# The gate product of the first half of each row tile: GpSimd in place of VectorE, in the transition behind the dilated attention

## The chip, the cores and the metric

The kernel runs on one core of one Trainium2 chip. A core has five engines with queues of their own: TensorE (PE in the profile, its weight loads PEld), VectorE (DVE), ScalarE (ACT), GpSimd (POOL) and SyncE (SP), which here issues the DMAs. The metric is device time in microseconds for one execution, the median of several runs.

## The reference

The kernel computes two decoder layers on a sequence of 512 rows of width 1024 in float32. Each layer is feed-forward, token mixer, feed-forward; the mixer of layer 0 is latent attention, that of layer 1 is dilated attention. Every one of the six sub-layers is wrapped in the same way:

```
hn = rmsnorm(x, pre_g) * (1 + scale) + shift
y  = rmsnorm(fn(hn), post_g)
x  = x + res_w * gate * y
```

So at the end of a sub-layer each row of its output y needs the mean of its squares, a product with the 1024 gates (gate, post_g and res_w folded into one row), a factor of its own (the inverse root of that mean) and a sum with x. Then the next sub-layer's norm takes the mean of squares of the new x, and its inverse root. The change touches the product with the gates alone.

## The kernel before, in words

Every float32 weight or activation that enters a matmul is split into a high part (ScalarE) and a low part (VectorE, a subtraction), and three matmuls make up one product (`mm3`, lines 149 to 151). The lines of these splits are 134 and 136 for weights (67 and 71 where they come in two halves) and 711 and 712 for the last attention outputs.

Rows are cut into four tiles of 128 (i = 0 to 3), the width into two halves of 512 (d = 0, 1). A transition between two sub-layers goes through the tiles in order:

- `tail(i)` has TensorE do the last products of tile i, for both halves, in PSUM; `y_part` adds them on VectorE to the part made earlier (line 465), into `y[i][d]` in SBUF.
- `y_done(i, d)` squares the half on ScalarE with a sum over the row (line 316), and multiplies the half in place by the gates `gb` (line 477, VectorE). The square reads y before the product overwrites it.
- `tile_done(i)`: `scale_of` adds the two sums on VectorE (line 323) and raises the result to the power -0.5 on GpSimd (line 324, 128x1). Then VectorE does x = y * r + x for both halves (line 505).
- `normal(i)`: both halves of the new x are squared (line 316), the same `scale_of` follows, and the normed rows are written by ScalarE (half 0, line 339) and VectorE (half 1, line 340).
- `turn`: for each pair of tiles, TensorE transposes the normed rows (line 529), and `modulate` scales and splits them on VectorE and ScalarE (lines 311 to 313; two columns out of eight by ScalarE and GpSimd, lines 307 to 309). The first matmuls of the next sub-layer need these.

Around the transition, ScalarE and VectorE also split the first weights of the next feed-forward sub-layer.

The program is written with a framework that traces the instructions, plans their order on each engine by priorities and cost estimates of its own, and sets the semaphores. `high_priority(offset=HOT)` (400) raises the steps of `y_part` and `y_done`, twice that those of `scale_of`. In the dilated sub-layer's main part the order of TensorE, ScalarE and VectorE is the written one; in the transition behind it only that of SyncE is, and the other four queues are planned. On each engine instructions run in the planned order.

`busy` is a class attribute: True for the dilated mixer alone, False for the latent one; the feed-forward class calls `y_done` on its own. In `Mixer.tail` the step of the change is the last line:

```python
t.y_part(i, d, b, False)
t.y_done(i, d)
```

Of the kernel before, what the change touches and what calls it, by code (L numbers as in the profile page):

```python
# [10 lines left out]
ALU = mybir.AluOpType  # L11
# [4 lines left out]
SEQ = 512  # L16
# [60 lines left out]
class Trunk:  # L77
# [390 lines left out]
            else:  # L468
                nc.scalar.activation(y, b, AF.Copy)

    def y_done(self, i, d):
        with self.tc.high_priority(offset=HOT):
            if d == 0:
                self.ss = self.pair()
            y = self.y[i][d]
            self.square(y, self.t("sq", SB), self.ss[:, d : d + 1])
            self.nc.vector.tensor_tensor(y, y, self.gb[:, d * SEQ : (d + 1) * SEQ], ALU.mult)

    def transition(self, sub, nxt):
        for u in (sub, nxt):  # L480
# [57 lines left out]
class Ffn:  # L538
# [89 lines left out]
    def tail(self, i):  # L628
        self.down(len(GROUPS) - 1, i)
# [34 lines left out]
class Mixer:  # L664
# [30 lines left out]
    def tail(self, i):  # L695

        t = self.t
        if i == 0:
            self.open = {(q, d): t.bank() for q in range(self.waiting) for d in range(2)}
            for (q, d), b in self.open.items():  # L700
                self.products(b, q, d, range(self.early, KT - 1))
        for d in range(2):
            b = self.open.get((i, d)) or t.bank()
            self.products(b, i, d, range(KT - 1 if (i, d) in self.open else self.early, KT))
            t.y_part(i, d, b, False)
            t.y_done(i, d)

    def put_o(self, src):
        t, nc = self.t, self.t.nc
# [915 lines left out]
```

## Time and profile before

| quantity | value |
|---|---|
| median of 3 runs (lowest, highest) | 2249.92 us (2248.58, 2249.99) |
| the profiled execution's own time | 2249.64 us |
| its span in the trace | 2247.9 us |
| TensorE busy, granted clock | 2217.0 us (99%), 0.997 |
| VectorE busy | 1181.0 us (53%) |
| ScalarE busy | 847.8 us (38%) |
| GpSimd busy | 108.6 us (5%) |

The profile is that of one execution. The transition behind the dilated sub-layer lies at about 1855 to 1890 us of its span. A row of the timeline has the start in us, the length in us, engine, line, operation, output<-inputs, shapes and a count; in brackets stands how long the engine sat idle before it, and what ended that. Two instructions that follow each other on VectorE or ScalarE overlap by some 0.08 to 0.1 us, so the distance from start to start is shorter than the length.

### The profile page before, as it was taken

How to read it: one execution, taken by the hardware profiler on the slowest of the kernel's cores; microseconds unless marked ns; L12 is line 12 of the kernel's file. 1: busy time of each engine (PE TensorE's matmuls, PEld its weight loads, DVE VectorE, ACT ScalarE, POOL GpSimd, SP SyncE). 2: the span in 40 equal slices, each digit the busy share in tenths (PEclk: the TensorE clock that was granted, in tenths of full speed). 3: DMA queues.
4: the chain of work that ended last, by engine and by line, in shares of the span. 5: the costliest groups of instructions: out<-in, count | busy, mean ns of one | idle time of the engine just before them, and what ended most of it. 6: DMA issues, size and time to landing. Idle time of an engine off the chain costs nothing.

```text
span 2247.9 us, 30150 instructions
## 1 busy us (share of the span) xinstructions
PE 2217.0 (99%) x11354; PEld 1868.2 (83%) x11354; DVE 1181.0 (53%) x2691; ACT 847.8 (38%) x1730; POOL 108.6 (5%) x143
## 2 busy tenths in 40 slices
PE   7999999999999999999999999999999999999998
PEld 5888888877898888898888889888899888888887
DVE  7666565677665456574554464234523457333344
ACT  4432234578633132353222353425442446322232
POOL 0000001210110000020000010000000002000000
PEclk9999999999999999999999999999999999999999
DMA  8575762311155365434644523323342334233231
GB/s 309 161 243 185 199 216 74 108 55 57 61 167 185 113 180 178 138 111 132 190 167 133 159 92 108 111 90 97 85 130 68 104 81 143 90 118 100 77 112 38
DMA packets 124058, 290.34 MB, mean 129 GB/s; under 512 B 44787, under 2 KB 49158, under 8 KB 123911
## 3 DMA queue, kind: packets, MB, share of 16 engines
q1 hardware_dynamic: 123910, 288.41, 40.8%
q8 instruction: 89, 1.46, 0.3%
q14 instruction: 59, 0.48, 0.1%
HBM read 281.76 MB, written 4.49 MB: 127 GB/s over the span
## 4 chain that ended last, share of the span: by engine, by line
PE 89%; ACT 2%; DVE 2%; issue 2%; DMA 2%; POOL 1%; SPq 1%; POOLq 0%; DVEq 0%; ACTq 0%
PE mm L149 28%; PE mm L150 28%; PE mm L151 27%; PE mm L882 1%; PE aux L1297 1%; PE mm L1130 1%; PE aux L931 1%; PE aux L1264 1%; POOL mv L324 1%; PE aux L910 1%; PE aux L529 0%; DVE wlo L136 0%; DMA z<-dz 0%; ACT whi L134 0%; DMA d<-w 0%
## 5 line engine op out<-in xcount | busy, mean ns | idle before, releaser
L136 DVE TENSOR_TENSOR wlo<-raw,whi 128x512 fp32r<-128x512 f32 (+1 forms) x714 | 466.1, 690 | 593.1 <-ACT whi L134 588.9
L149 PE MATMUL mm<-s,whi 128*128 128x512 f32 (+1 forms) x1932 | 722.6, 375 | 1.5 <-ACT whi L134 1.5
L150 PE MATMUL mm<-s,whi 128*128 128x512 f32 (+1 forms) x1932 | 719.1, 372 | 0.0
L151 PE MATMUL mm<-s,wlo 128*128 128x512 f32 (+1 forms) x1932 | 718.7, 372 | 0.0
L134 ACT ACTIVATE whi<-raw 128x1024 fp32r<-128x1024 f32 (+1 forms) x357 | 369.3, 1048 | 786.5 <-PE mm L150 540.7
L149 PEld LDWEIGHTS mm<-s,whi 128*128 128x128 f32 x1932 | 364.6, 189 | 68.9 <-issue 3.5
L151 PEld LDWEIGHTS mm<-s,wlo 128*128 128x128 f32 x1932 | 364.5, 189 | 63.6
L150 PEld LDWEIGHTS mm<-s,whi 128*128 128x128 f32 x1932 | 364.8, 189 | 61.8
L149 PE MATMUL mm<-whi,s 128*128 128x512 f32 (+1 forms) x1040 | 406.4, 391 | 1.7 <-ACT s L711 1.7
L150 PE MATMUL mm<-wlo,s 128*128 128x512 f32 (+1 forms) x1040 | 404.4, 389 | 0.0
L151 PE MATMUL mm<-whi,s 128*128 128x512 f32 (+1 forms) x1040 | 404.2, 389 | 0.0
L149 PEld LDWEIGHTS mm<-whi,s 128*128 128x128 f32 x1040 | 210.8, 203 | 37.2 <-ACT s L711 2.1
L151 PEld LDWEIGHTS mm<-whi,s 128*128 128x128 f32 x1040 | 210.8, 203 | 34.5 <-DVE s L712 0.2
L150 PEld LDWEIGHTS mm<-wlo,s 128*128 128x128 f32 x1040 | 210.9, 203 | 33.8 <-issue 0.3
L171 DVE CUSTOM_DVE_ANT_0 raw<-raw,cs 128x1024 f32<-128x1024 f32 x130 | 160.0, 1235 | 123.2 <-DMA raw<-w_mod 122.6
L465 DVE TENSOR_TENSOR s<-mm,s 128x512 f32<-128x512 f32 x112 | 76.6, 689 | 119.0 <-PE mm L151 118.8
L324 POOL TENSOR_TENSOR mv<-mv,mhalf 128x1 f32<-128x1 f32 x48 | 36.1, 755 | 1486.9 <-DVE mv L323 1484.4
L1095 ACT ACTIVATE s<-mm 128x128 f32<-128x128 f32 (+3 forms) x109 | 33.2, 360 | 165.2 <-PE mm L151 161.3
L588 ACT ACTIVATE s<-gg 128x512 fp32r<-128x512 f32 (+1 forms) x97 | 57.4, 592 | 44.8 <-DVE gg L587 44.8
L587 DVE TENSOR_TENSOR gg<-silu,mm 128x512 f32<-128x512 f32 (+1 forms) x95 | 59.8, 629 | 9.3 <-ACT silu L585 9.3
L585 ACT ACTIVATE silu<-mm 128x512 f32<-128x512 f32 (+1 forms) x95 | 51.4, 541 | 18.1 <-PE mm L151 18.1
L1211 ACT ACTIVATE u<-u,y 128x128 f32<-128x128 f32 x128 | 49.6, 397 | 22.1 <-DVE y L1189 10.0
(185 smaller groups left out, 1686.4 us busy)
## 6 DMA issues: line engine op xcount, KB each, us to landing
raw<-w_gu SPq DMA_DIRECT2D x168, 512.0 KB, 4.2
raw<-w_mod SPq DMA_DIRECT2D x130, 512.0 KB, 4.6
raw<-w_down SPq DMA_DIRECT2D x88, 512.0 KB, 4.4
raw<-dil_in SPq DMA_DIRECT2D x47, 512.0 KB, 4.1
raw<-dil_v SPq DMA_DIRECT2D x20, 512.0 KB, 4.5
s<-w_mod SPq DMA_DIRECT2D x28, 256.0 KB, 6.0
raw<-w_gu SPq DMA_DIRECT2D x16, 256.0 KB, 3.8
raw<-mla_o SPq DMA_DIRECT2D x8, 512.0 KB, 3.9
```

The lines of the kernel that those rows point to most:

```text
L134: self.nc.scalar.activation(hi, raw, AF.Copy)
L136: self.nc.vector.tensor_tensor(lo[:, r], raw[:, r], f(hi[:, r]), ALU.subtract)
L149: mm(out, w[0], m[0], start=first, stop=False)
L150: mm(out, w[0], m[1], start=False, stop=False)
L151: mm(out, w[1], m[0], start=False, stop=last)
L171: nc.vector.tensor_tensor_reduce(raw, raw, self.cs, 1.0, 0.0, ALU.mult, ALU.add, accum_out=t[:, 0:1])
L324: nc.gpsimd.tensor_tensor(v[:, 1:2], v[:, 0:1], self.mhalf[:, 0:1], ALU.pow)
L465: nc.vector.tensor_tensor(y, b, y, ALU.add)
L585: nc.scalar.activation(s, banks[0], AF.Silu)
L587: nc.vector.tensor_tensor(v, s, banks[1], ALU.mult)
L588: nc.scalar.activation(ghi, v, AF.Copy)
L1211: nc.scalar.activation(c, c, AF.Exp, bias=pair["top"][:, g, i, one], scale=-1.0, accum_out=pair["z"][:, g, i, one],)
```

## The change

`y_done` gets a flag, and with it the product with the gates is issued on GpSimd in place of VectorE. `Mixer.tail` sets it for half 0 where `busy` is true, which is the dilated mixer: four instructions of 128x512 in all, one for each row tile. Half 1 and everything else stays.

```diff
-    def y_done(self, i, d):
+    def y_done(self, i, d, spare=False):
         with self.tc.high_priority(offset=HOT):
             if d == 0:
                 self.ss = self.pair()
             y = self.y[i][d]
             self.square(y, self.t("sq", SB), self.ss[:, d : d + 1])
-            self.nc.vector.tensor_tensor(y, y, self.gb[:, d * SEQ : (d + 1) * SEQ], ALU.mult)
+            eng = self.nc.gpsimd if spare else self.nc.vector
+            eng.tensor_tensor(y, y, self.gb[:, d * SEQ : (d + 1) * SEQ], ALU.mult)
...
             t.y_part(i, d, b, False)
-            t.y_done(i, d)
+            t.y_done(i, d, self.busy and d == 0)
```

## Rows read from the trace of the kernel before

**Rows 1.** The page: busy time of the engines over the whole span, and the share of each in the chain that ended last.

```profile
PE 2217.0 (99%) x11354; PEld 1868.2 (83%) x11354; DVE 1181.0 (53%) x2691; ACT 847.8 (38%) x1730; POOL 108.6 (5%) x143
...
PE 89%; ACT 2%; DVE 2%; issue 2%; DMA 2%; POOL 1%; SPq 1%; POOLq 0%; DVEq 0%; ACTq 0%
```

**Rows 2.** Busy time in stretches of the transition: the stretch, its length, then busy us (and instructions) of PE, PEld, DVE, ACT and POOL, the granted clock of TensorE, the DMA share and GB/s.

```profile
1860.00:1870.00 10.00, 10.00 (x47) 8.28 (x46) 9.84 (x18) 8.75 (x22) 1.57 (x3) 1.00 0.43 150
1870.00:1880.00 10.00, 5.67 (x32) 5.03 (x31) 9.76 (x23) 9.27 (x22) 4.26 (x5) 0.83 0.39 126
...
1878.00:1879.00 1.00, 1.00 (x7) 1.00 (x6) 1.00 (x3) 1.00 (x4) 0.53 (x1) 0.50 0.73 246
1879.00:1880.00 1.00, 1.00 (x7) 1.00 (x7) 1.00 (x3) 1.00 (x4) 1.00 (x1) 0.61 0.02 8
```

**Rows 3.** Timeline of TensorE: the two instructions of 1860 to 1890 us before which it sat idle.

```profile
1872.04 1.53 PE L529 MATMUL aux<-ident,s 128*128 128x128 f32 x12 [1.64 <-ACT s L339]
1876.27 0.73 PE L149 MATMUL mm<-s 128*128 128x256 f32 x2 [2.69 <-ACT s L312]
```

**Rows 4.** Groups of VectorE's instructions from 1855 to 1890 us: the product with the gates (busy us, mean ns).

```profile
L477 DVE TENSOR_TENSOR s<-s,gb 128x512 f32<-128x512 f32 x8 | 5.2, 684 | 0.0
```

**Rows 5.** Timeline of VectorE in the transition, tiles 0 to 2.

```profile
1859.21 0.15 DVE L323 SCALAR_TENSOR_TENSOR mv<-ss 128x1 f32<-128x1 f32 x1
1859.28 0.68 DVE L477 TENSOR_TENSOR s<-s,gb 128x512 f32<-128x512 f32 x1
1859.88 0.68 DVE L465 TENSOR_TENSOR s<-mm,s 128x512 f32<-128x512 f32 x1
1860.48 1.41 DVE L505 SCALAR_TENSOR_TENSOR x<-s,mv,x 128x512 f32<-128x512 f32 x2
...
1862.40 0.68 DVE L71 TENSOR_TENSOR s<-raw,s 128x512 fp32r<-128x512 f32 x1
1863.00 1.28 DVE L477 TENSOR_TENSOR s<-s,gb 128x512 f32<-128x512 f32 x2
1864.21 0.22 DVE L323 SCALAR_TENSOR_TENSOR mv<-ss 128x1 f32<-128x1 f32 x2
1864.51 0.69 DVE L465 TENSOR_TENSOR s<-mm,s 128x512 f32<-128x512 f32 x1
...
1867.60 0.69 DVE L465 TENSOR_TENSOR s<-mm,s 128x512 f32<-128x512 f32 x1
1868.20 0.69 DVE L136 TENSOR_TENSOR wlo<-raw,whi 128x512 fp32r<-128x512 f32 x1
1868.80 1.29 DVE L477 TENSOR_TENSOR s<-s,gb 128x512 f32<-128x512 f32 x2
1870.00 0.22 DVE L323 SCALAR_TENSOR_TENSOR mv<-ss 128x1 f32<-128x1 f32 x2
```

**Rows 6.** Timeline of ScalarE in the same stretch: the squares of half 0 of tiles 0, 1 and 2, the normed rows of tile 1, and the first high parts for the next sub-layer.

```profile
1857.59 0.63 ACT L316 ACTIVATE sq<-s 128x512 f32<-128x512 f32 x1 [2.10 <-DVE s L465]
...
1861.88 0.62 ACT L316 ACTIVATE sq<-s 128x512 f32<-128x512 f32 x1
...
1867.37 0.62 ACT L316 ACTIVATE sq<-s 128x512 f32<-128x512 f32 x1
...
1871.27 0.72 ACT L339 ACTIVATE s<-x,mv 128x512 f32<-128x512 f32 x1 [0.50 <-POOL mv L324]
...
1875.82 0.71 ACT L312 ACTIVATE s<-u 128x256 fp32r<-128x256 f32 x2
```

**Rows 7.** Timeline of GpSimd in the same stretch: all it does there up to 1876 us.

```profile
1859.44 0.93 POOL L324 TENSOR_TENSOR mv<-mv,mhalf 128x1 f32<-128x1 f32 x1 [95.53 <-DVE mv L323]
1864.43 1.20 POOL L324 TENSOR_TENSOR mv<-mv,mhalf 128x1 f32<-128x1 f32 x2 [4.07 <-DVE mv L323]
1870.24 1.62 POOL L324 TENSOR_TENSOR mv<-mv,mhalf 128x1 f32<-128x1 f32 x2 [4.61 <-DVE mv L323]
```

**Rows 8.** GpSimd elsewhere: the group of the products with sines in the latent attention (same shape and type; count, busy us, mean ns), and one subtraction of half the width behind the transition.

```profile
L830 POOL TENSOR_TENSOR s<-s 128x512 f32<-128x512 f32 x4 | 5.1, 1283 | 69.1 <-DVE s L828 64.1 <-issue 5.0
...
1903.94 0.74 POOL L590 TENSOR_TENSOR s<-gg,s 128x256 fp32r<-128x256 f32 x1 [5.08 <-ACT s L588]
```

**Rows 9.** Timelines of GpSimd and VectorE at two other places where both work on SBUF at once: at 54 us (GpSimd 128x512), and at 993 us (GpSimd 128x256).

```profile
54.54 0.68 DVE L190 CUSTOM_DVE_ANT_0 s<-s,cs 128x512 f32<-128x512 f32 x1
55.15 1.78 DVE L190 CUSTOM_DVE_ANT_0 s<-s,cs 128x512 f32<-128x512 f32 x1
54.84 1.54 POOL L309 TENSOR_TENSOR s<-u,s 128x512 fp32r<-128x512 f32 x1 [11.84 <-ACT u L308]
...
993.88 0.68 DVE L136 TENSOR_TENSOR wlo<-raw,whi 128x512 fp32r<-128x512 f32 x1
994.48 1.21 DVE L171 CUSTOM_DVE_ANT_0 raw<-raw,cs 128x1024 f32<-128x1024 f32 x1
995.63 1.75 DVE L171 CUSTOM_DVE_ANT_0 raw<-raw,cs 128x1024 f32<-128x1024 f32 x1
993.55 2.75 POOL L590 TENSOR_TENSOR s<-gg,s 128x256 fp32r<-128x256 f32 x1 [2.77 <-ACT s L588]
```

**Rows 10.** Timeline of SyncE's queue behind the last product: the gates of the next sub-layer, then the next weights.

```profile
1876.05 0.33 SPq L246 DMA_DIRECT2D gb<-row  x1
1879.53 4.91 SPq L124 DMA_DIRECT2D raw<-w_gu  x2
```

## The prediction

> **What bounds the kernel now.** I read the page first: TensorE is busy in 2217.0 of 2247.9 us and holds 89% of the chain that ended last [rows 1]. So a change that adds or removes no matmul counts only where TensorE stands. I then went to the one place where the four products lie, and cut it into stretches: from 1860 to 1870 us TensorE is full, from 1870 to 1880 it works 5.67 of 10 us, while VectorE is at 9.84 and 9.76 and ScalarE at 8.75 and 9.27 [rows 2]. Here VectorE and ScalarE set the pace. TensorE's own timeline shows the two waits: 1.64 us until the normed rows of tile 1 are written by ScalarE, and 2.69 us until the first high part for the next sub-layer is there, together 4.33 us [rows 3]. Behind the second wait the granted clock is at its lower level, 1.2 GHz (0.50 in 1878 to 1879), and returns during 1879 to 1880 [rows 2]; from the restart at 1876.27 to about 1879.7 half the time, some 1.7 us, is lost as well. So 4.33 + 1.7 = 6.0 us is the most that any repair of this place can win.
>
> What releases the first wait can be followed backwards in the timelines: the normed rows (1871.27) stood behind a power on GpSimd (1870.24) [rows 6, 7], that behind the tiny sum of line 323 on VectorE (1870.00), and that behind the two gate products of tile 2 (1868.80) [rows 5]. The same pattern stands at tile 1: two products at 1863.00, the sum at 1864.21, the power at 1864.43 [rows 5, 7].
>
> **The change part by part.**
>
> *Removed from VectorE.* Four products of 128x512. One lasts 684 ns [rows 4], but two in a row take 1.20 us from the first's start to the next instruction (1868.80 to 1870.00 [rows 5]), so a place in the queue is worth 0.60 us, four 2.4 us. Only those of tiles 1 and 2, 1.2 us, stand directly ahead of a sum on the way to the restart. Tile 0's would give 0.6 more if all behind it moved up. Tile 3's lies behind the work that releases TensorE and is worth nothing.
>
> *Added on GpSimd.* Four products with three operands in SBUF. The nearest row has the same shape, type and operation: 1283 ns [rows 8]. So one product is 0.6 us longer than on VectorE (1.28 against 0.68), and GpSimd has the time: between 1859 and 1876 it did nothing but powers [rows 7]. Two costs follow.
>
> *The power behind the product.* The product can start when the square of half 0 is done. ScalarE starts it at 1857.59, 1861.88 and 1867.37 for tiles 0 to 2, 0.62 us each [rows 6]; the square of half 1 follows within a further 0.8 us or less (0.61 and the reading of the sum), and then the power could run. In GpSimd's queue it stands behind a product of 1.28 us. With nothing else in the way it is late by 1.28 - 0.8 = 0.5 us a tile. What waits for the power is line 505, and through it everything of that tile.
>
> *VectorE and GpSimd at the same memory.* At 54.84 us GpSimd runs a 128x512 subtraction. The VectorE instruction that starts at 55.15 takes 1.78 us in place of the 0.68 of its neighbour and ends 0.55 us after GpSimd does (56.93 against 56.38): it stood still until GpSimd was through. GpSimd too was stretched, to 1.54 us, while VectorE's earlier instruction finished [rows 9]. At 993.55 us VectorE runs without a gap, and a GpSimd instruction of half our width takes 2.75 us in place of 0.74 [rows 8, 9]: it waited some 2.0 us before it got its turn, and then VectorE's instruction took 1.75 for 1.21 us.
>
> The Trainium skill states this as a lock (SBUF — State Buffer, "Who interferes with whom"): a VectorE instruction with two SBUF inputs and a GpSimd instruction that reads SBUF take the shared port pair for the whole instruction, and the second to issue blocks. The first half agrees with the 1.78 us [rows 9]; by the page GpSimd would wait for one VectorE instruction, by the row at 993.55 it waited for several. With one such wait of 0.69 us at tiles 1 and 2 the sum would be 2 x (0.69 + 1.28 - 0.60) = 2.7 us slower, 2252.3.
>
> So the 0.60 us that VectorE saves can be lost again: its remaining product, the sums and lines 71, 136 and 505 read two operands from SBUF. Line 465 reads one from PSUM; no row of before shows it beside a GpSimd product. From both sides: if it runs on, 0.60 of the 1.28 us are covered where it comes at the right moment; if not, nothing is. I take that it runs on. For one tile VectorE's balance is then between -0.60 (nothing stops) and 1.28 - 0.60 = +0.68 us (all stops).
>
> *The sum, tile by tile.* Tile 0: product on GpSimd from about 1858.35 to 1859.65. VectorE's product of half 1 stands until then and ends its place at 1860.25, line 465 at 1860.85, and line 505 starts there in place of 1860.48 [rows 5]: +0.4. Tile 1: ScalarE's square starts 0.4 later and ends at 1862.9. GpSimd comes in behind line 71, at 1863.4, and is through at 1864.7. VectorE's product of half 1 takes until 1865.3, the power starts at 1865.5 in place of 1864.43 [rows 5, 7]: +1.1. Tile 2: the square ends at about 1868.7 (ScalarE had 0.3 us of other work to spare), just under line 465, so GpSimd gets in at 1868.75 and ends at 1870.05. Line 136 and the product of half 1 follow, two places of 0.60, and the power that was at 1870.24 starts at 1871.4 to 1871.5: +1.2. From there to the restart ScalarE's queue runs without a gap [rows 2], so TensorE's two waits end some 1.2 us later. For tile 3 up to 0.5 us more falls on low parts behind the restart; I take 0.1. Sum: +1.3 us.
>
> *What moves besides.* No DMA moves. SyncE's queue is passed by one wait: the load of the next gates (1876.05) must wait for the last product that reads the old ones. Behind it stand weight loads, issued at 1879.53 [rows 10], 3.5 us later; a delay of 1 to 2 us is covered by that, beyond 3.5 us it would be paid. Priorities and the planner's estimate for the new engine can also swap neighbours in the planned queues; I cannot price that but by the ends of the range.
>
> The profiled execution took 2249.64 us, 1.74 above its span. Plus 1.3: 2250.9; its distance to the median (2249.92) is 0.3, so 2251.0 it is. A difference of 0.2%, 4.5 us, is about what a measurement of this kernel can tell from no change; the forecast lies well inside.
>
> **The rivals.**
>
> *A, the forecast: stalls eat more than the saving.* +0.4 to +2.6 us, 2250.0 to 2252.3, chance 0.45. Against it: the planner may put line 465 or waits under each product.
>
> *B, relief.* GpSimd works beside VectorE, and the sums of line 323 move up. For it: the products stand directly ahead of those sums, and VectorE is full. Against it: [rows 9]. Price: 1.2 us from tiles 1 and 2, 1.8 with tile 0: 2247.8 to 2248.4; chance 0.22. If the second wait also shrank enough for the clock to stay up, up to 4.5 us or more could go, 2245; of the 0.22 I give that 0.03.
>
> *C, slower by more: GpSimd cannot get in.* Place: between the lines 465 of tile 1 (1864.51) and of tile 2, VectorE's queue is a row of two-operand instructions. If GpSimd waits for the next gap, as at 993.55, it waits for line 71, a product and two sums (1.3 us) at tile 1, and for line 136, a product, sums and line 71 (1.9 us) at tile 2; the power stands behind. Price: (1.3 + 1.28 - 0.60) + (1.9 + 1.28 - 0.60) = 4.6 us at most, 2254.2; 3 us, 2252.6 and more, in part. It decides from a wait of about 0.7 us each. For it: the 2.0 us. Against it: VectorE soon waits for squares, and each wait is a gap. Chance 0.18, of which 0.05 beyond 4.5 us.
>
> *D, nothing.* The saved places and stalls cancel (0.60 against 1.28 with a line 465 of 0.60 beside it: 0.08 a tile), or the planner's order changes so that the powers go first. -0.6 to +0.4 us, 2249.0 to 2250.0, chance 0.12. *E:* the planner reorders far behind the transition, either sign, 0.03, 0.02 of it slower.
>
> **How the numbers follow.** Faster by over 0.2%: 0.03 of B. Slower: 0.05 of C and 0.02 of E, 0.07. The rest is 0.90. The forecast's own range is 2250.0 to 2252.3. For 8 in 10 it is drawn out over D, the plain part of B and the lower half of C: 2247.6 to 2253.6.
>
> **What would show it.** Right: products of line 477 on GpSimd of 1.28 us and more; VectorE instructions beside them well over 0.69 us; the powers of line 324 later against the squares; TensorE's two waits together at 5 to 6.5 us in place of 4.33. B is shown by waits under 3.5 us and no long instruction on VectorE; C by products over 2 us with line 505 waiting for them. The forecast is wrong if the waits of TensorE there shrink, or if the time moves while they stay.

## The result, and the profile after

The changed kernel takes 2253.03 us (median of 22 runs, 2251.33 to 2255.34), the kernel before 2249.92 (22 runs, 2248.01 to 2252.29). The ratio is 1.0013, 95% interval 1.0007 to 1.0019, so 1.6 to 4.3 us slower with 3.1 in the middle. That is inside the 0.2% that the prediction counted as no change and inside its wide range (2247.6 to 2253.6), but more than twice the 1.3 us of its forecast, and above the forecast's own range (2250.0 to 2252.3). The profiled execution took 2252.72 us, with a span of 2250.9 and a granted clock of 0.996. Behind the change every line number of the code is one higher: the product is line 478, the sum with x 506, the transposes 530, the last splits 712 and 713.

The busy times of the page, after (before is in [rows 1]):

```profile
PE 2217.9 (99%) x11354; PEld 1868.6 (83%) x11354; DVE 1181.3 (52%) x2687; ACT 848.2 (38%) x1730; POOL 114.5 (5%) x147
```

Four instructions went from VectorE to GpSimd (2691 to 2687 and 143 to 147). VectorE is nevertheless no less busy than before, 1181.3 us against 1181.0: what it saved it spends in longer instructions elsewhere.

Busy time of the changed kernel by stretches, with the columns of [rows 2]:

```profile
1860.00:1870.00 10.00, 8.86 (x41) 6.97 (x40) 9.18 (x15) 8.69 (x21) 3.77 (x4) 1.00 0.31 110
1870.00:1880.00 10.00, 5.99 (x33) 4.79 (x34) 8.60 (x20) 7.95 (x17) 4.98 (x6) 0.88 0.30 87
...
1880.00:1881.00 1.00, 1.00 (x6) 1.00 (x6) 1.00 (x2) 0.90 (x3) 0.66 (x1) 0.50 0.88 348
...
1883.00:1884.00 1.00, 1.00 (x7) 1.00 (x7) 1.00 (x4) 1.00 (x2) 0.03 (x2) 0.50 0.73 123
```

VectorE gets through 15 and 20 instructions in the two long stretches where it had 18 and 23 [rows 2], at less busy time: its instructions are longer, and it waits more. The granted clock is at its lower level, 1.2 GHz (0.50), still at 1883 to 1884, in place of up to 1879.7 before. TensorE's restart behind the last attention output lies 1.4 us earlier than before (1854.17 against 1855.54), ahead of everything the change touches, so places are compared below by their distance from it.

TensorE's timeline: the restart behind the last attention output, and the waits of the transition, as in [rows 3]:

```profile
1854.17 0.50 PE L149 MATMUL mm<-whi,s 128*128 128x512 f32 x1 [1.95 <-ACT s L712]
...
1872.04 1.54 PE L530 MATMUL aux<-ident,s 128*128 128x128 f32 x12 [3.18 <-DVE s L340]
...
1875.15 0.50 PE L149 MATMUL mm<-s 128*128 128x256 f32 x2 [1.34 <-ACT s L312]
...
1877.41 0.30 PE L530 MATMUL aux<-ident,s 128*128 128x128 f32 x1 [0.38 <-ACT s L339]
```

The first wait grew from 1.64 to 3.18 us, the second shrank from 2.69 to 1.34, a third of 0.38 is new: 4.90 us in place of 4.33. The length of these waits is that of one execution only; two other traces of the same order show 2.05 us for the first (below).

GpSimd's timeline, with the four products and the powers ([rows 7] before):

```profile
1857.02 1.29 POOL L478 TENSOR_TENSOR s<-s,gb 128x512 f32<-128x512 f32 x1 [94.73 <-ACT sq L316]
1858.41 0.93 POOL L324 TENSOR_TENSOR mv<-mv,mhalf 128x1 f32<-128x1 f32 x1
...
1861.64 1.30 POOL L478 TENSOR_TENSOR s<-s,gb 128x512 f32<-128x512 f32 x1 [2.30 <-ACT sq L316]
1863.64 1.11 POOL L324 TENSOR_TENSOR mv<-mv,mhalf 128x1 f32<-128x1 f32 x2 [0.70 <-DVE mv L323]
...
1867.21 1.35 POOL L478 TENSOR_TENSOR s<-s,gb 128x512 f32<-128x512 f32 x1 [2.45 <-ACT sq L316]
1870.46 1.56 POOL L324 TENSOR_TENSOR mv<-mv,mhalf 128x1 f32<-128x1 f32 x2 [1.90 <-DVE mv L323]
...
1874.26 1.28 POOL L478 TENSOR_TENSOR s<-s,gb 128x512 f32<-128x512 f32 x1 [2.24 <-ACT sq L316]
1875.69 0.60 POOL L324 TENSOR_TENSOR mv<-mv,mhalf 128x1 f32<-128x1 f32 x1 [0.16 <-DVE mv L323]
...
2244.50 0.86 POOL L324 TENSOR_TENSOR mv<-mv,mhalf 128x1 f32<-128x1 f32 x1 [7.29 <-DVE mv L323]
```

Every product waits for the square alone and then runs its 1.28 to 1.35 us: GpSimd gets in nearly at once. At tiles 0, 1 and 3 VectorE was then at an instruction that reads from PSUM (lines 465 and 311); at tile 2 line 71, with two operands in SBUF, still ran for 0.20 us, and that product is the longest, 1.35 us. Only at tile 0 does the power stand directly behind the product (1858.31 to 1858.41). Even there it starts 0.07 us behind the end of VectorE's sum (1858.34), as in the kernel before (1859.36 and 1859.44). At tiles 1 to 3 GpSimd is idle again, for 0.70, 1.90 and 0.16 us, and waits for VectorE's sum.

VectorE's timeline, the instructions beside those products ([rows 5] before):

```profile
1857.59 0.75 DVE L323 SCALAR_TENSOR_TENSOR mv<-ss 128x1 f32<-128x1 f32 x1 [0.27 <-ACT sq L316]
...
1862.22 1.28 DVE L478 TENSOR_TENSOR s<-s,gb 128x512 f32<-128x512 f32 x1 [0.15 <-ACT sq L316]
...
1867.32 1.79 DVE L136 TENSOR_TENSOR wlo<-raw,whi 128x512 fp32r<-128x512 f32 x1
...
1874.44 0.68 DVE L465 TENSOR_TENSOR s<-mm,s 128x512 f32<-128x512 f32 x1
1875.04 0.51 DVE L323 SCALAR_TENSOR_TENSOR mv<-ss 128x1 f32<-128x1 f32 x1
```

Four of them are long (0.75 for 0.15, 1.28 for 0.68, 1.79 for 0.68 and 0.51 for 0.15 us), and each starts inside a product. The two tiny sums end with it (1858.34 against 1858.31, 1875.55 against 1875.54), the two wide ones 0.55 us behind it (1863.50 against 1862.94, 1869.11 against 1868.56), as in [rows 9]. Together VectorE stood 0.60 + 0.60 + 1.11 + 0.36 = 2.67 us, against the 2.4 us that four places were worth. Line 465, which reads one operand from PSUM, ran its 0.68 us in the middle of the fourth product.

SyncE's timeline: the load of the next gates and the next weight load ([rows 10] before):

```profile
1878.61 0.33 SPq L246 DMA_DIRECT2D gb<-row  x1
1882.45 4.93 SPq L124 DMA_DIRECT2D raw<-w_gu  x2
```

The load of the gates is 2.6 us later (3.9 counted from TensorE's restart), and the weight load still lies 3.8 us behind it.

### The profile page after: what moved, and what is told of

Read it like the earlier page. It is cut to its first block, busy times and chain, and to the rows that moved or that the text cites. A ratio compares the mean times of both kernels' runs of the same rounds, so it can differ in the third digit from the quotient of the medians.

```text
span 2250.9 us, 30154 instructions
## 1 busy us (share of the span) xinstructions
PE 2217.9 (99%) x11354; PEld 1868.6 (83%) x11354; DVE 1181.3 (52%) x2687; ACT 848.2 (38%) x1730; POOL 114.5 (5%) x147
## 4 chain that ended last, share of the span: by engine, by line
PE 92%; DVE 2%; ACT 2%; issue 2%; POOL 1%; DMA 1%; SPq 0%; POOLq 0%; DVEq 0%; ACTq 0%
PE mm L149 28%; PE mm L150 28%; PE mm L151 28%; PE mm L883 1%; PE aux L1298 1%; PE mm L1131 1%; PE aux L1265 1%; PE aux L932 1%; POOL mv L324 1%; PE aux L911 1%; PE aux L530 0%; DVE x L506 0%; PE aux L1131 0%; ACT whi L134 0%; DVE wlo L136 0%
```

## The experiments

Four theories stood for the 3.1 us. First, the stalls: VectorE stands while GpSimd's product reads SBUF. Within it one fork: the price could also be GpSimd's queue, in which the powers stand behind the products. Second, the order: with the product on another engine, the planner puts VectorE's, ScalarE's and TensorE's instructions into another order, and that order is the slower one. Third, the clock: behind the longer first wait some 7 us pass at the lower level. Fourth, the end: time is lost far behind the transition.

To separate the transition from the rest I read one distance in each profile. T runs from TensorE's restart behind the last attention output (1854.17 above) to the start of the last power on GpSimd (2244.50 above). The end runs from there to the end of the span. In the kernel before, T is 2242.60 - 1855.54 = 387.06 us and the end 5.30. Its two rows, of TensorE and of GpSimd:

```profile
1855.54 0.50 PE L149 MATMUL mm<-whi,s 128*128 128x512 f32 x1 [1.70 <-ACT s L711]
...
2242.60 0.86 POOL L324 TENSOR_TENSOR mv<-mv,mhalf 128x1 f32<-128x1 f32 x1 [7.29 <-DVE mv L323]
```

T is cut once more, at the twelve transposes that TensorE starts behind its first wait (1872.04 above); "ahead" is the part from the restart to them. The column on the clock gives the time within T at the lower level (0.50), and where it lies.

| kernel | T, us | ahead, us | at 0.50, us | end, us | timed: ratio to before [95%] |
|---|---|---|---|---|---|
| before | 387.06 | 16.50 | 3.4 behind | 5.30 | |
| before, again | 387.43 | 16.55 | 3.4 behind | 5.22 | |
| changed | 390.33 | 17.87 | 6.8 behind | 6.40 | 1.0013 [1.0007, 1.0019] |
| changed, again | 389.81 | 18.32 | 3.4 ahead | 6.30 | |
| changed, four VectorE fills at the start | 389.79 | 18.31 | 3.4 ahead | 5.26 | 1.0011 [1.0002, 1.0020] |
| before + a GpSimd product | 390.90 | 19.29 | 3.4 ahead, 3.4 behind | 5.25 | 1.0021 [1.0012, 1.0031] |
| before + two GpSimd fills | 387.46 | 16.54 | 3.4 behind | 5.26 | 1.0007 [0.9998, 1.0016] |
| changed, without the product | 386.86 | 15.64 | none | 6.37 | 1.0005 [0.9996, 1.0014] |
| the same, four VectorE fills at the start | 387.76 | 15.65 | 6.8 behind | 5.23 | 0.9999 [0.9990, 1.0008] |
| product moved in tile 3 only | 388.32 | 16.50 | 3.4 behind | 5.28 | 1.0008 [0.9999, 1.0016] |
| product moved in tiles 0 to 2 | 388.73 | 17.86 | 3.4 across | 5.24 | 1.0005 [0.9996, 1.0014] |
| before, sums raised | 391.41 | 15.10 | 10.2 behind | 5.52 | 1.0015 [1.0006, 1.0024] |
| before, weights split early | 390.31 | 18.63 | 6.8 ahead, 3.4 behind | 5.22 | 1.0016 [1.0007, 1.0025] |
| changed, weights split early | 389.70 | 18.82 | 6.8 ahead | 5.26 | 1.0016 [1.0007, 1.0026] |

**The two kernels again.** The kernel before with one unused line of Python, and the changed kernel as it is, each profiled once more.

> The kernel before once more, for how far the stretch repeats between executions: 387.06 us within 0.3, waits of TensorE of 1.64 and 2.69 us and 3.4 us at the lower clock, by all theories. If the stretch moves by more than 1 us, single traces do not tell the theories apart.

> The changed kernel once more: 390.33 us within 0.3, waits of 3.18, 1.34 and 0.38 us and about 7 us at the lower clock, by all theories. If the time at the lower clock differs from trace to trace while the order is the same, the clock's part of the loss is chance.

They took 2247.93 and 2252.37 us. T repeated within 0.4 us for the one and 0.5 for the other, a little more than the 0.3 expected. The changed kernel's first wait did not repeat:

```profile
1857.00:1858.00 1.00, 1.00 (x4) 0.81 (x3) 0.50 (x1) 0.87 (x3) 0.46 (x1) 0.50 1.04 397
...
1872.81 1.54 PE L530 MATMUL aux<-ident,s 128*128 128x128 f32 x12 [2.05 <-DVE s L340]
```

Here the lower clock lies directly behind the restart (1855.3 to 1858.7), TensorE's products take longer, and it waits less for the same rows. At tile 0 VectorE was then idle or at line 465 until the product's last 0.14 us, and none of its instructions stood; beside the other three products one stood as before, for 0.59, 1.10 and 0.35 us. So a wait's length says little by itself, and a difference of 1 us in T counts where the clock was low at the same place.

**A GpSimd product beside the order of before.** VectorE keeps all eight products. GpSimd multiplies the gates by themselves into the scratch tile of the square, which makes it wait for the square as the moved product does.

```diff
-            eng = self.nc.gpsimd if spare else self.nc.vector
-            eng.tensor_tensor(y, y, self.gb[...], ALU.mult)
+            if spare:
+                self.nc.gpsimd.tensor_tensor(s, g, g, ALU.mult)
+            self.nc.vector.tensor_tensor(y, y, g, ALU.mult)
```

> The kernel before, with all eight products still on VectorE, plus a product of the same shape on GpSimd (gates times gates, into the scratch tile of the square, which nobody reads) at the place where the change puts it. The planned order on TensorE, VectorE, ScalarE and SyncE is that of the kernel before; only GpSimd's queue has four more instructions. Theory 1 (stalls: the product holds up VectorE and the powers behind it): slower than before by 2 to 4 us, and the stretch from TensorE's restart behind the last attention output to the last power (387.06 us in the trace of before, 390.33 in that of the changed kernel) grows to 389 to 391. Theory 2 (the new planned order is what costs): as before, 387 us within 0.5. Theory 3 (TensorE's clock stays at its lower level for longer, whatever delays it): between, and the stretch grows by as much as the time at the granted clock of 0.50 adds.

The planned order of TensorE, VectorE, ScalarE and SyncE is that of before, instruction by instruction. T is 390.90 us, 3.65 above the mean of the two traces of the kernel before (387.25), and the timed kernel is 2.7 to 7.0 us slower (2 to 4 expected). VectorE's timeline:

```profile
1863.64 0.69 DVE L465 TENSOR_TENSOR s<-mm,s 128x512 f32<-128x512 f32 x1 [0.71 <-PE mm L151]
1864.25 1.05 DVE L71 TENSOR_TENSOR s<-raw,s 128x512 fp32r<-128x512 f32 x1
...
1870.34 1.53 DVE L136 TENSOR_TENSOR wlo<-raw,whi 128x512 fp32r<-128x512 f32 x1
```

and TensorE's:

```profile
1875.04 1.53 PE L533 MATMUL aux<-ident,s 128*128 128x128 f32 x12 [2.77 <-ACT s L339]
...
1879.26 0.51 PE L149 MATMUL mm<-s 128*128 128x256 f32 x2 [2.69 <-ACT s L312]
```

Two VectorE instructions of 0.68 us stand, for 0.37 and 0.85 us, ahead of the transposes. But not all of the 3.65 us is the product's. In this execution the lower clock lay behind the restart (1857.0 to 1860.4), and line 465 at 1863.64, which waited for TensorE, is 1.63 us later from the restart than its like before (1861.80 [rows 5]), with no VectorE instruction yet stopped. Without that, about 2 us are left, by an estimate from these rows. So with no product saved and no order changed the place loses most of what the whole change loses. The other order is not needed for the loss.

**Two GpSimd fills in the same place.** The fork between the stalls and GpSimd's queue: the product is replaced by instructions that take GpSimd nearly as long, ahead of the same powers, but read nothing from SBUF.

```diff
+            if spare:
+                for _ in range(2):
+                    self.nc.gpsimd.memset(s, 0.0)
+            self.nc.vector.tensor_tensor(y, y, self.gb[...], ALU.mult)
```

> The kernel before with all eight products on VectorE, plus, where the extra GpSimd product stood, two GpSimd fills of 128x512 with a constant (into the scratch tile of the square): about as long together as the extra product (1.04 us), in the same queue ahead of the same powers, but they read nothing from SBUF. Planned order of the other queues as before. Theory 1a (what costs is that VectorE's instructions with two SBUF operands stand while GpSimd reads): the stretch from TensorE's restart to the last power is as before, 387.2 us within 0.5, and no instruction of VectorE beside the fills is longer than 0.75 us. Theory 1b (what costs is the power standing behind the product in GpSimd's queue): the stretch grows as with the extra product (390.9), to 389 or more.

GpSimd's, VectorE's and TensorE's timelines of this kernel, one after the other:

```profile
1861.18 1.11 POOL L480 MEMSET sq<- 128x512 f32 x2 [2.29 <-ACT sq L316]
```

```profile
1860.98 0.68 DVE L71 TENSOR_TENSOR s<-raw,s 128x512 fp32r<-128x512 f32 x1
1861.58 1.29 DVE L481 TENSOR_TENSOR s<-s,gb 128x512 f32<-128x512 f32 x2
```

```profile
1870.62 1.53 PE L533 MATMUL aux<-ident,s 128*128 128x128 f32 x12 [1.64 <-ACT s L339]
...
1874.84 0.51 PE L149 MATMUL mm<-s 128*128 128x256 f32 x2 [2.69 <-ACT s L312]
```

The two fills take 1.11 us together. Beside them VectorE's instructions keep their 0.68 us (1.29 for a pair), TensorE's two waits are 1.64 and 2.69 us as in [rows 3], and T is 387.46, as before. So what costs is what the product has and the fills have not, the reading of SBUF first of all, and 1.11 us more in GpSimd's queue costs nothing. This agrees with the Trainium skill (SBUF — State Buffer, "Who interferes with whom"): a VectorE instruction with two SBUF inputs contends with a GpSimd instruction that reads SBUF, and not with one that only writes it.

**The changed kernel without the moved product.** The four products are left out, on both engines, so the first half of y is not multiplied by the gates.

```diff
-            eng = self.nc.gpsimd if spare else self.nc.vector
-            eng.tensor_tensor(y, y, self.gb[...], ALU.mult)
+            if not spare:
+                self.nc.vector.tensor_tensor(y, y, self.gb[...], ALU.mult)
```

> The changed kernel with the four products of half 0 left out altogether (the output lacks the gates there). The planned order on TensorE, VectorE, ScalarE and SyncE is that of the changed kernel. Theory 1 (stalls): as fast as before or up to 1.8 us faster, the stretch at 385.3 to 387. Theory 2 (the new order costs): as slow as the changed kernel, 390 us within 0.5. Theory 3 (clock): decided by whether the granted clock falls to 0.50 during the first matmuls of the next sub-layer: if it stays there 7 us as in the changed kernel, slower than before by about 1.8 us even with no stall.

The planned order of TensorE, VectorE, ScalarE and SyncE is exactly that of the changed kernel. With it all four combinations are there: in the order of before T is 387.25 without and 390.90 with a product on GpSimd (some 1.6 of that difference the clock's), in the order of the changed kernel 387.3 (the mean of 386.86 and 387.76, below) without and 390.0 with it. Where the clock was low at the same place, 6.8 us behind the transposes, it is 387.76 without and 390.33 with the product: 2.6 us. TensorE's timeline here:

```profile
1870.81 1.54 PE L530 MATMUL aux<-ident,s 128*128 128x128 f32 x12 [0.95 <-DVE s L340]
...
1873.97 0.50 PE L149 MATMUL mm<-s 128*128 128x256 f32 x2 [1.39 <-ACT s L312]
...
1876.15 0.33 PE L530 MATMUL aux<-ident,s 128*128 128x128 f32 x1 [0.60 <-ACT s L339]
...
1877.42 0.39 PE L150 MATMUL mm<-s 128*128 128x256 f32 x1 [0.35 <-DVE s L313]
...
1879.20 0.39 PE L150 MATMUL mm<-s 128*128 128x256 f32 x1 [0.44 <-POOL s L309]
...
1880.35 0.39 PE L151 MATMUL mm<-s,wlo 128*128 128x256 f32 x1 [0.41 <-DVE wlo L136]
```

T is 386.86 us, that of before: the order by itself costs nothing. But it wins nothing either, although four of VectorE's products are gone without any price. The first wait shrank to 0.95 us, and five others took its place, for ScalarE, VectorE and GpSimd in turn: 0.95 + 1.39 + 0.60 + 0.35 + 0.44 + 0.41 = 4.14 us in all, against 4.33. The transposes do come 0.9 us sooner (15.64 against 16.50), and behind them most or all of that is lost again (371.22 us, and 372.11 below, against 370.56 and 370.88). A part of it is seen: in this order line 506 of tile 3 meets a GpSimd subtraction of line 309 that the kernel before has too, and the two instructions take 1.9 us for 1.4, with and without the moved product. In this order the saving that the change was to bring has a ceiling of nothing; the order of before without the products was not run.

The two traces also show where the product costs at equal order: from the restart to the power of tile 2 are 14.07 us here and 16.29 in the changed kernel (1870.46 - 1854.17), and to the transposes 15.64 and 17.87, 2.2 us more. Behind the transposes it costs 0.3 to 0.4 more (372.46 against 372.11 with 6.8 us at the lower clock there, 371.49 against 371.22 with none).

**The end.** The page shows one end of 6.3 to 6.4 us where the others have 5.2 to 5.3, in the changed kernel and in the one without the product. DMA from 2243 us to the end, first the changed kernel, then the kernel before; the lines give queue and kind, packets, MB and the share of the 16 engines:

```profile
q1 hardware_dynamic: 288, 0.52, 10.8%
q14 instruction: 1, 0.01, 0.1%
```

```profile
q1 hardware_dynamic: 288, 0.52, 10.6%
```

Behind the last outputs lies a transfer of the kind "instruction" that the kernel before has at about 2228 us. The changed kernel, in both its traces, and the one without the product have it, and four VectorE instructions fewer (2687 against 2691). So four were given back, as fills of 128x1 at the very start, far from the place.

```diff
-        nc.vector.memset(self.mhalf, -0.5)
+        for _ in range(5):
+            nc.vector.memset(self.mhalf, -0.5)
```

> The changed kernel with four tiny fills more on VectorE at the very start (0.1 us each, a constant written again), so that VectorE has as many instructions as in the kernel before; planned order else as in the changed kernel. Theory 4 (the four instructions that left VectorE's program shift a fetch of instructions to the end of the execution): the time from the last power to the end of the span, 6.35 us in both traces of the changed kernel and 5.2 to 5.3 before, is 5.3 again, and no DMA of the kind instruction lies behind the last output; the total is about 1 us under the changed kernel's. If the end depends on something else that the change moved: 6.35 as before, same total.

> The kernel without the four products of half 0 (left out altogether), and with the four tiny fills on VectorE at the start. It shows what the change could have won at best: four places on VectorE free, nothing on GpSimd, no shifted fetch at the end. If the saving is as small as the first such trace said: stretch 386.9 us within 0.4, end 5.3 us, total 0.2 to 0.6 us under before, that is no difference the timing can tell. If the first trace was a lucky or unlucky one: a stretch of 385.5 us would say that the prediction's 1.2 to 1.8 us are there to be had, 388 that the new order costs.

DMA of the padded changed kernel from 2235 us to the end:

```profile
q1 hardware_dynamic: 576, 1.05, 13.2%
```

The late transfer is gone, and the end is 5.26 and 5.23 us in the two padded kernels: it is worth 1.1 us in the traces. The timed medians move the same way, from 1.0013 to 1.0011 and from 1.0005 to 0.9999, but these intervals overlap, so by the times alone it isn't shown. Which engine's code is fetched the trace doesn't say, and the count isn't the whole rule: the kernel with the raised sums (below) has as many VectorE instructions as before, such a transfer at 2232 us, ahead of the last outputs, and an end of 5.52; with one and three VectorE instructions fewer (the product moved in one or three tiles, below) no such transfer lies behind the last outputs, and the changed kernel with the weights split early has 2687 and an end of 5.26.

**The clock.** The same order ran in three profiles of the changed kernel with the clock in different states. The first has 0.50 from about 1877.6 to 1884.4 us. The second, at the same place:

```profile
1880.00:1881.00 1.00, 1.00 (x9) 0.82 (x7) 0.91 (x2) 0.48 (x2) 0.63 (x2) 1.00 0.80 295
...
1883.00:1884.00 1.00, 1.00 (x10) 0.93 (x9) 1.00 (x3) 0.45 (x4) 0.78 (x1) 1.00 0.31 127
```

The clock stayed up there, and TensorE did 19 matmuls in these two microseconds in place of 13, and waited 0.38, 0.54, 0.45 and 0.42 us behind its restart at 1875.92. From the transposes to the last power are 372.46 us in the first trace and 371.49 and 371.48 in the two others. The pair without the product says the same: 371.22 with the clock up, 372.11 with 6.8 us at the lower level. So 6.8 us at the lower level cost 0.9 to 1.0 us here, and not the half of their length: where VectorE and ScalarE set the pace, a slower TensorE mostly fills its own waits. Directly behind TensorE's restart, where VectorE waits for TensorE's products, 3.4 us at that level made line 465 1.63 us late (above), nearly the half. The third theory falls as the main cause: it accounts for 1.0 of the 3.3 us by which T grew in the first trace, and the other two, with the clock up at that place, still have T at 389.8.

**Tile by tile.** The product moved in tile 3 alone, and in tiles 0 to 2.

```diff
-            t.y_done(i, d, self.busy and d == 0)
+            t.y_done(i, d, self.busy and d == 0 and i == 3)
```

> The change for row tile 3 alone: one product on GpSimd in place of four. The prediction said that tile 3's product lies behind the work that releases TensorE. Theory 1 (stalls ahead of TensorE's restart): waits of TensorE of 1.64 and 2.69 us as before, stretch 387.2 us plus at most 0.5; total within 1.5 us of before. Theory 2 (the new order costs): depends on how far the order moved with one product; it moved little, so within 0.5 us as well. More than 2 us slower would say that stalls behind the restart cost too.

> The change for tiles 0, 1 and 2, tile 3's product back on VectorE. Tile 3 alone grew the stretch by 1.1 us; if the parts add up, this one has 390.07 - 1.1 = 389.0 us within 0.5. If it is as long as with all four (390), tile 3's product is hidden behind the others; if near 387.5, tile 3 was the only one that counts. VectorE's instructions beside the products stand as in the changed kernel.

Tile 3 costs 388.32 - 387.25 = 1.1 us in T, more than the 0.5 expected, and all of it behind the transposes, which start 16.50 us from the restart as before. Tiles 0 to 2 cost 1.5, of which 1.3 ahead of them (17.86). 1.1 + 1.5 = 2.6 against 2.7 for the mean of the three traces with all four tiles: the sums agree within what T repeats, though the planned order of VectorE is another one in each of these kernels. By the timed ratios alone neither differs from before. Tile 3 alone, GpSimd's, VectorE's and TensorE's timelines:

```profile
1874.01 1.78 POOL L478 TENSOR_TENSOR s<-s,gb 128x512 f32<-128x512 f32 x1 [2.90 <-ACT sq L316]
```

```profile
1874.59 1.75 DVE L478 TENSOR_TENSOR s<-s,gb 128x512 f32<-128x512 f32 x1
```

```profile
1875.52 0.51 PE L149 MATMUL mm<-s 128*128 128x256 f32 x2 [2.69 <-ACT s L312]
...
1876.87 0.39 PE L150 MATMUL mm<-s 128*128 128x256 f32 x1 [0.61 <-DVE s L313]
```

GpSimd's product comes 0.02 us behind the start of line 136 on VectorE (1873.99, 0.68 us) and waits for it: 1.78 us in place of 1.28. Then VectorE's product of half 1 stands 1.07 us (1.75 for 0.68), the low part of line 313 comes behind it, and TensorE has restarted on the high part at 1875.52 and runs dry 0.61 us for that low part.

**Tries at a faster version.** First, the sums of the dilated transition raised in priority, in the kernel before, so that VectorE takes them ahead of the weight splits:

```diff
-            self.tile_done(nxt, i)
+            with self.tc.high_priority(offset=HOT if getattr(sub, "busy", False) else 0):
+                self.tile_done(nxt, i)
```

> A try to win what the change was after: the kernel before, all products on VectorE, but the sums with x and the norm behind them (lines 505, 316, 339, 340) raised in priority by as much as the products, in this transition only, so that the planner puts splits of weights (lines 67, 71, 134, 136) behind them. If the waits of TensorE (4.33 us) come from VectorE's and ScalarE's order: they shrink, 1 to 3 us faster. If these engines' sheer load sets them: same within 1 us. If the splits come too late now: TensorE waits for them behind the restart, slower by up to 3 us.

```profile
1869.07 1.53 PE L530 MATMUL aux<-ident,s 128*128 128x128 f32 x12 [0.88 <-ACT s L339]
...
1872.83 0.33 PE L530 MATMUL aux<-ident,s 128*128 128x128 f32 x1 [1.53 <-ACT s L339]
...
1875.96 0.80 PE L149 MATMUL mm<-s 128*128 128x256 f32 x2 [2.80 <-ACT s L312]
...
1878.46 0.58 PE L150 MATMUL mm<-s 128*128 128x256 f32 x1 [1.28 <-DVE s L313]
```

TensorE's timeline shows a first wait cut to 0.88 us and waits that only moved on (1.53, 2.80 and 1.28 us), the last two for the high and low parts of the normed rows (lines 312 and 313). The transposes come 1.4 us sooner (15.10), the rest takes 5.6 us more with 10.2 us at the lower clock, and T is 391.41, 4.2 above before.

Second, the first weights of the next sub-layer loaded and split before the transition, in the dilated part, on the kernel before and on the changed one:

```diff
-            if nxt and i == 1:
+            if nxt and i == 1 and not sub.parks:
                 nxt.prepare()
...
             self.norm(last)
+            w = [Sliced(t, t.a["w_gu"][self.nxt.l, self.nxt.s, 0, g]) for g in range(2)]
+            self.nxt.w[0] = [x.parts() for x in w]
+            for x in w:
+                for j in range(2):
+                    x.fetch(j)
...
                 t.unpark(i)
+            for x in w:
+                for j in range(2):
+                    x.top(j)
+                    x.low(j)
```

> A try that follows from the runs so far: the four instructions that VectorE and ScalarE spend on the split of the next sub-layer's first weights (lines 67 and 71) are moved out of the transition, ahead of it, where both sit idle (ScalarE 13.39 us until 1854.86, VectorE 5.85 us until 1854.07 in the trace of before); their loads start behind the last exponentials. All products on VectorE. If the load of the two engines between the restart and 1888 us sets the time: 4 x 0.60 = 2.4 us less on each, TensorE's waits of 4.33 us shrink by 1 to 2.4 us, total 1 to 2.4 us under before. If the planner fills the room with later splits (line 136) ahead of the norm, or the chain of square, sum and power sets the time: within 0.5 us of before. If the loads get in the way of those that the last attention output waits for: TensorE's restart comes later by 1 us or more and the total with it.

> The kernel of early_split with the change on top (four products on GpSimd). Theory 1 (VectorE stands while GpSimd reads): the stretch is longer than early_split's by 2 to 3.5 us, as it was between the changed kernel and the one without its products (3.2). If with less load on VectorE the products fall into gaps: by less than 1 us.

On the kernel before, the restart's own wait grew from 1.70 to 3.79 us, as the third branch of the expectation said, and behind it 6.8 us pass at the lower clock, in the other kernel of the pair too (3.71 us). This trace is of the slowest execution of the kernel (2256.23 us, median 2252.77). With the product on GpSimd VectorE stands as in the changed kernel, 0.58 us at a line 136 (1867.16) and 0.60 at a line 478 (1873.70) ahead of the transposes. And yet the ratio is the same, 1.0016, and T isn't longer: it is 0.6 us shorter (389.70 against 390.31). The 2 to 3.5 us that the stalls were to cost here did not come. Ahead of the transposes, with 6.8 us at the lower clock in both, the two differ by 0.2 us (18.63 and 18.82). That VectorE waits for TensorE's products there, so that a stall falls into a wait, is one reading. The planned order is another one too, so the reason is open. No version beat the kernel before.

## Why the prediction was right, and where its size was off

*What bounds the place* was right: TensorE waits for VectorE and ScalarE, and what changes there changes the time.

*The product on GpSimd, 1.28 us*: 1.28 to 1.35 measured. *VectorE's two-operand instructions stand until it is through*: four did in the first trace, for 2.67 us, three in the second, and *line 465 runs on* held at the fourth product. Of the four signs named three came: the products' length, long instructions on VectorE, and later powers, as the power of tile 2 at 16.29 us behind the restart where it was at 14.70 (1870.24 - 1855.54). The fourth did not: TensorE's two waits were to be 5 to 6.5 us, and they were 4.52, with the new third one 4.90; in the second trace the two are 3.38, less than before, where the prediction said that shrinking waits would show it wrong. The clock moves these waits from one execution to the next, so they were a bad sign to choose; T was not.

*The power late behind the product by 0.5 a tile* was wrong. At tile 0 too it started where VectorE's sum let it, and more work in GpSimd's queue was free (the two fills). The powers were late because VectorE's sums were, and those because VectorE stood.

*Tiles 0 to 2, +1.2 us* at TensorE's waits: the transposes came 1.37 us later (17.87 against 16.50), so this term was right. Its steps were 0.4, 1.1 and 1.2; line 505 of tile 0 came 0.35 us later, the powers of tiles 1 and 2 0.58 and 1.59. At tile 1 the named product stood; at tile 0 it was a sum, and at tile 2 line 136.

*Tile 3 and what lies behind the restart, +0.1 us*, is the term that was mis-sized. From the transposes to the last power the changed kernel takes 371.5 to 372.5 us, depending on the clock, against 370.6 and 370.9 before. The restart of TensorE isn't the end of the place: its low parts and the other half's rows still come from the same VectorE, and the new third wait, 0.38 us for the rows of line 339, shows that TensorE has no store of work there. Tile 3's product moved alone costs 1.1 us there. How much of it is tile 3's in the changed kernel is open: at equal order the four products cost only 0.3 to 0.4 there, and the rest stands there without them too.

*What moves besides* priced swapped neighbours by the ends of the range, and the order as a whole indeed cost nothing in T: 0.9 us less ahead of the transposes, and 0.5 to 1.4 more behind them, depending on the clock. But nothing in it reaches the end of the program, and there the second missing term lies: an instruction transfer, 1.1 us in the traces. By the tiles moved apart the sum is 1.5 + 1.1 + 1.1 = 3.7 us, against 3.1 timed [1.6 to 4.3]. The profiled spans differ by 3.0: 3.3 in T and 1.1 at the end, less the 1.4 us by which TensorE's restart happened to lie earlier.

*The clock, some 1.7 us lost behind the second wait*, was too much: 0.9 to 1.0 us for a stretch twice as long. With it "the most that any repair can win", 6.0 us, was too high.

*SyncE's queue*: the load of the gates came 3.9 us later from the restart, beyond the 3.5 us that the prediction called covered, and the weight load behind it came 4.3 later. None of TensorE's waits there is for a load, so no price of it is seen.

*The last sum*: 2249.64 + 1.3 is 2250.9, and with the 0.3 to the median 2251.2, not 2251.0. In C, the line 465 at 1864.51 is the sixth of eight and so tile 2's, not tile 1's; its price doesn't use it.

*Rival B, relief*, is out from two sides: the stalls eat 2.67 of 2.4 us, and without any stall the four places are worth nothing in the new order (386.86 and 387.76 against 387.06 and 387.43). Its 1.2 us took the first wait's last releaser for the only one. *Rival C, GpSimd cannot get in*, got the size nearly right with the wrong mechanism: in the changed kernel GpSimd waited for VectorE once, for 0.07 us by the longest product, and it was VectorE that stood. That was decided by what VectorE happened to run when each square ended; tile 3 moved alone met line 136 and waited 0.50 us. *Rival D, nothing*, falls with the interval above 1. *Rival E, another order*: the planner did reorder, and without the product that order takes what the old one takes.

So the mechanism was the forecast's, stalls that eat more than the saving, but its number was not: 2253.0 lies where the prediction had put rival C (2252.6 and more). That the wide range held it is luck, since it was drawn over C's lower half for another reason.

## What to carry to other kernels

A product moved from VectorE to GpSimd is not off VectorE while it runs there: look, for each, for two-operand SBUF instructions that VectorE has queued beside it. Here each product stopped one such instruction for up to 1.11 us, unless VectorE was idle or at one that reads PSUM (tile 0 of the second trace); and with the weights split early the stalls were there and no loss was seen. Before pricing a saving, ask what the place would do if the work were free: here leaving the four products out altogether won nothing: the transposes came 0.9 us sooner, and what stands behind them, a chain of square, sum and power over three engines, gave it back. That this chain is the reason is argued, not shown. To tell a lock from a queue, replace the suspected instruction by one of like length that reads nothing. And before two traces are compared, see where in each the clock was low.

## What was not expected of the hardware

- Four VectorE instructions fewer moved a transfer of the kind "instruction" from about 2228 us to behind the last outputs, and the end of the program grew from 5.3 to 6.3 us; four idle fills at the start took it back.
- Two GpSimd fills of 128x512 take 1.11 us together and disturb no VectorE instruction, where a product of 1.28 us stopped one in seven cases out of eight (two traces of the changed kernel).
- 6.8 us at the granted clock of 0.50 cost 0.9 to 1.0 us where VectorE and ScalarE set the pace; 3.4 us of it where VectorE waits for TensorE made VectorE 1.63 us late.
- The same two engines blocked each other in both directions: a product that came when VectorE was at an instruction with two SBUF operands waited for it (0.50 us at tile 3 alone), and then stopped the next one.
